# The first loads of a two-layer encoder trunk split over two DMA queues, with matmuls of ones ahead of its first product

## The chip, the core and the metric

The kernel runs on one core of one Trainium2 chip. The metric is the device time of one execution in microseconds (us). Three runs of the kernel before the change took 1084.82, 1081.86 and 1082.02 us, so the median is 1082.02 us. A further execution was recorded by the hardware profiler; it took 1083.18 us, of which 1081.4 us are the span from its first to its last instruction, so that 1.78 us lie around the span.

## What is computed

Two layers of an encoder over 256 tokens with 1024 channels. Each layer applies a gated feed-forward block, a mixer with two groups of heads (neighbourhood attention and a gated long convolution), a second feed-forward block and an input embedding that goes through a gate. The change touches only what happens ahead of, and in, the first feed-forward block of the first layer:

```python
def swiglu(h, w_gate, w_up, w_down):
    return (jax.nn.silu(h @ w_gate) * (h @ w_up)) @ w_down

for i in range(DEPTH):
    x = x + 0.5 * swiglu(rmsnorm(x, g_ffa[i]), w_ffa_gate[i], w_ffa_up[i], w_ffa_down[i])
    u = rmsnorm(x, g_mix[i]) @ w_in[i]
    ...
return rmsnorm(x, g_final)
```

## The kernel before

**Layout.** Channels lie on the 128 partitions and tokens along the free axis. The input x is eight chunks of 128 channels by 256 tokens, 128 KB each, in tiles `x0` to `x7`. Every weight of both layers comes as one long stream of pieces of 1 MB, `w[n]`, each holding 16 tiles of 128x128. A piece is loaded into a `raw` buffer (three of them) by `load()`, and is then cut in two halves of eight tiles by `part()`. The first four pieces are called w0, w1, w2 and so on here.

**Two products for one.** Each weight and each activation is split into a rounded part and a rest. ACT makes the rounded part of a weight half (`wh`, line L281), and DVE subtracts it from the raw weights to get the rest (`wl`, L283). For the input, ACT multiplies chunk c by its gain (`xg`, L1193) and DVE writes the rest behind it (L1196). PE then does one matmul of `wh` with both parts of the activation side by side (512 columns, L188) and, later, one of `wl` with the rounded part alone (256 columns, L197). Six buffers each hold `wh` and `wl`, so ACT and DVE run at most six halves ahead of PE.

**The first block.** The first four halves (w0 and w1) hold the tiles of four output blocks at once, in the order of the chunks: a quarter of a piece is the four tiles that belong to one chunk. PE does eight matmuls of L188 for two chunks, then eight of L197 for the same, four times over. Then come w2, w3, w4 and so on with two output blocks each, 16 matmuls of L188 and 16 of L197 a piece.

**The norm.** The division by the root mean square is applied after the product. ACT squares the eight chunks (L348), POOL adds the squares into `acc` in seven additions, one after the other (L351), and PE sums over the partitions with four small matmuls (L413). DVE takes the sums from there (L421) into a chain of small operations that ends in two scaled identity matrices (L428 feeds ACT's L433), and PE spreads the result over the partitions at L436.

**What sets the order.** PE and ACT run in the order in which the program is written: a fibre per piece of side work is advanced after every few matmuls. The order on DVE, POOL and SP is chosen by a scheduler when the kernel is built. All engines run their own rows strictly in order. All loads are issued from SP's queue. A load takes one of eight completion semaphores in turn, and waits until the load that used it before has landed, so eight loads can be under way.

**The lines to follow.** SP issues the gains and other small columns (`sm`, L251), then w0 in quarters (L253) with `x0` to `x3` between them (L254), then `x4` to `x7` (L257, L259) around two halves of w1 (L258), then whole pieces (L261). ACT's first work is the load of a table for its functions and a dummy activation (L223). The loop at L1188 to L1196 writes the first eight chunks' work in order.

Of the kernel before, what the change touches and what calls it, by code (L numbers as in the profile page):

```python
# [11 lines left out]
F32 = mybir.dt.float32  # L12
# [6 lines left out]
P = 128  # L19
T = 256  # L20
D = 1024
DEPTH = 2
KD = D // P
# [4 lines left out]
EPS = 1e-6  # L28
HALF = 8
GROUP = 24  # L30

E = mybir.EngineType
ORDERED = {E.PE,E.Activation}
# [44 lines left out]
def hybrid_trunk(ctx: ExitStack, tc: tile.TileContext, w, xT, pT, rpb, small, gfin, wf, zT, dft, idft, decay, out):  # L78
    nc = tc.nc
    V, S, G, PE = nc.vector, nc.scalar, nc.gpsimd, nc.tensor  # L80

    cp = ctx.enter_context(tc.tile_pool(name="const", bufs=1))
# [13 lines left out]
    def nm(s):  # L96
        uid[0] += 1
        return f"{s}{uid[0]}"
# [4 lines left out]
    def t2(dt=F32, s="t"):  # L103
        return k2.tile([P, 512], dt, tag="k2", name=nm(s))
# [7 lines left out]
    def f(ap):  # L112
        return ap.bitcast(F32)
# [66 lines left out]
    class Wide:  # L180
# [6 lines left out]
        def mm(cls, b, lh, ll, r, start, stop, last):  # L187
            PE.matmul(b, lh, r, start=start, stop=False)  # L188
            cls.later.append((b[:, T:], ll, r[:, :T], stop))
            if last or len(cls.later) == GROUP:  # L190
                cls.flush()
# [18 lines left out]


    sm = cp.tile([P, DEPTH * NCOL], F32, name="sm")
    x = [cp.tile([P, T], F32, name=f"x{c}") for c in range(KD)]

    def col(i, c):
        return sm[:, i * NCOL + c : i * NCOL + c + 1]
# [2 lines left out]
    V.memset(onesf, 1.0)  # L219
    ones = cp.tile([P, P], F32R, name="ones")  # L220
    V.tensor_copy(ones, onesf)
    warm = sp.tile([P, 2], F32, tag="warm", name="warm")
    S.activation(warm, onesf[:, 0:2], AF.Silu)  # L223
    ident = cp.tile([P, P], F32, name="ident")
# [19 lines left out]
    def load():  # L244
        n = Stream.loaded
        if n >= DEPTH * PIECES:
            return
        raw = rawp.tile([P, 16, P], F32, tag="raw", name=nm("raw"))
        src = w[n].rearrange("p (a b) -> p a b", b=P)
        if n == 0:  # L250
            nc.sync.dma_start(sm, small)  # L251
            for q in range(4):
                nc.sync.dma_start(raw[:, 4 * q : 4 * q + 4], src[:, 4 * q : 4 * q + 4])  # L253
                nc.sync.dma_start(x[q], xT[q])  # L254
        elif n == 1:
            for q in range(2):
                nc.sync.dma_start(x[4 + 2 * q], xT[4 + 2 * q])  # L257
                nc.sync.dma_start(raw[:, q * HALF : (q + 1) * HALF], src[:, q * HALF : (q + 1) * HALF])  # L258
                nc.sync.dma_start(x[5 + 2 * q], xT[5 + 2 * q])  # L259
        else:  # L260
            nc.sync.dma_start(raw, src)  # L261
        Stream.raws[n] = raw
        Stream.loaded += 1

    def part(steps=1):

        n = Stream.parted
        Stream.parted += 1
        while Stream.loaded < min(n // 2 + 2, DEPTH * PIECES):
            load()  # L270
        raw = Stream.raws[n // 2]
        h = whp.tile([P, HALF, P], F32R, tag="wh", name=nm("wh"))
        l = wlp.tile([P, HALF, P], F32R, tag="wl", name=nm("wl"))
        fb = Fiber(None)
        Stream.ready[n] = (h, l, fb)

        def go():
            k = HALF // steps
            for a in range(0, HALF, k):
                src = raw[:, n % 2 * HALF + a : n % 2 * HALF + a + k]  # L280
                S.copy(h[:, a : a + k], src)  # L281
                yield
                V.tensor_sub(l[:, a : a + k], src, f(h[:, a : a + k]))  # L283
            if n % 2:
                Stream.raws.pop(n // 2)
                load()

        fb.gen = go()
        return fb
# [892 lines left out]


    load()
    load()
    first = [part(2), part(2), part(), part()]
    hls = [t2(F32R, "xg") for _ in range(KD)]
    for c in range(KD):  # L1188
        g = col(0, C_FFA + c)
        fb = first[c // 2]  # L1190
        if c % 2 == 0 or c < 4:
            fb.step()
        S.activation(hls[c][:, :T], x[c], AF.Copy, scale=g)  # L1193
        if c % 2:
            fb.finish()
        V.scalar_tensor_tensor(hls[c][:, T:], x[c], g, f(hls[c][:, :T]), op0=ALU.mult, op1=ALU.subtract)  # L1196
# [24 lines left out]
def _constants():  # L1221


    n = 2 * T
    ang = 2.0 * np.pi * (np.outer(np.arange(T), 2 * np.arange(P) + 1) % (2 * n)) / (2 * n)
    re, im = np.cos(ang), -np.sin(ang)
    dft = np.concatenate([re, im], axis=1).reshape(P, 2, T).transpose(1, 0, 2).astype(np.float32)
    sign = 1.0 - 2.0 * (np.arange(T) % 2)
    idft = (np.stack([re.T, re.T * sign, im.T, im.T * sign]) * (2.0 / n)).astype(np.float32)

    tl = np.linspace(0.0, 1.0, T, dtype=np.float32)
    wv = (np.float32(2.0 * math.pi) * np.arange(T, dtype=np.float32) / np.float32(T)).astype(np.float32)
    fb = np.linspace(1e-4, 15.0, 16, dtype=np.float32)
    fw = (fb[None, :] * wv[:, None]).astype(np.float32)
    order = np.arange(T).reshape(P, 2).T.ravel()
    zT = np.zeros((P, T), np.float32)
    zT[:33] = zT[64:97] = np.concatenate([tl[:, None], np.cos(fw), -np.sin(fw)], axis=1)[order].T
    deltas = np.abs(np.linspace(math.log(1e-2) / 1.5, math.log(1e-2) / 0.3, HY, dtype=np.float32))
    decay = np.exp(-tl[:, None] * deltas[None, :]).astype(np.float32)[order].reshape(2, P, HY)
    return dft, idft, zT, decay  # L1240


def _rpb_index():

    r, c = np.arange(T) // 64, np.arange(T) % 64
    lo = np.clip(c - 8, 0, 48)[:, None]
    ok = (c[None] >= lo) & (c[None] < lo + 16)
    at = (r[None] - r[:, None] + 7) * 31 + np.clip(c[None] - c[:, None] + 15, 0, 30)
    return np.where(ok, at, 15 * 31).reshape(2, P, T).transpose(1, 0, 2)
# [49 lines left out]
def _layout(a):  # L1299
    small = np.zeros((P, DEPTH * NCOL), np.float32)  # L1300

    def cols(v):
        return v.reshape(-1, P).T

    for i in range(DEPTH):
        b = i * NCOL
        for c, name in ((C_FFA, "g_ffa"), (C_MIX, "g_mix"), (C_OUT, "g_out"), (C_FFB, "g_ffb"), (C_PLE, "g_ple")):
            small[:, b + c : b + c + 8] = cols(a[name][i])
        for j in range(3):
            small[:, b + C_SC + 12 * j : b + C_SC + 12 * (j + 1)] = cols(a["w_sc"][i, j])  # L1310
        small[:, b + C_BSC : b + C_BSC + 12] = cols(a["b_sc"][i])
        small[:, b + C_HYB : b + C_HYB + 4] = cols(a["hy_bias"][i])
        for j, name in enumerate(("b_f1", "b_f2", "b_f3", "filt_freq")):
            small[:64, b + C_BF + j] = small[64:, b + C_BF + j] = a[name][i]
    wf = np.zeros((DEPTH, P, 3 * P + 2 * HY), np.float32)
    for i in range(DEPTH):
        for j, name in enumerate(("w_f1", "w_f2", "w_f3")):
            v = a[name][i]
            for r in (0, 64):
                for c in (j * P, j * P + 64):  # L1320
                    wf[i, r : r + len(v), c : c + 64] = v
        wf[i, :64, 3 * P :] = wf[i, 64:, 3 * P :] = a["w_f4"][i]
    padded = np.full((DEPTH, NH, 15 * 31 + 1), -1e30, np.float32)
    padded[:, :, :-1] = a["na_rpb"].reshape(DEPTH, NH, 15 * 31)
    rpb = padded[:, :, _rpb_index()]
    dft, idft, zT, decay = _constants()
    return {
        "w": _weights(a),
        "xT": a["x"][0].T.reshape(KD, P, T),
        "pT": a["p"][:, 0].transpose(0, 2, 1),  # L1330
        "rpb": rpb,
        "small": small,
        "gfin": np.broadcast_to(a["g_final"], (P, D)),
        "wf": wf,
        "zT": zT,
        "dft": dft,
        "idft": idft,
        "decay": decay,
    }
# [17 lines left out]
```

## Time and profile before

The profile gives the busy time of each engine in the span, the share of what ended last, and the memory traffic:

| what | value |
|---|---|
| median of three runs | 1082.02 us |
| profiled execution | 1083.18 us |
| its span | 1081.4 us |
| DVE busy | 875.0 us (81%) |
| ACT busy | 659.4 us (61%) |
| POOL busy | 129.9 us (12%) |
| moved from memory | 192.38 MB, 179 GB/s over the span |
| PE's first matmul | 6.77 us after the start of the span |

An engine that is busy all the time is not by that alone the bound, since a matmul counts as busy while it streams at whatever rate the clock allows. So the rows to read beside the busy time are those of waits: which engine stood idle, before which line, and whose end released it. In the timeline, a row is a run of equal instructions: start, busy time, engine, line, what is written and read, and how many.

### The profile page before, as it was taken

The numbers are of one execution on the slowest core, as the hardware profiler recorded it, in microseconds if no ns is written. First come the engines' busy times: TensorE is split into PE (matmuls) and PEld (weight loads), VectorE is DVE, ScalarE is ACT, GpSimd is POOL, SyncE is SP. The second block draws the span as 40 slices with busy tenths as digits, with TensorE's granted clock in tenths as the row PEclk, the third lists the DMA queues.
The fourth block names the chain that finished last, engine by engine and source line by source line (L and its number), as shares of the span: only waits on it lengthen the run. The fifth ranks groups of instructions, "written<-read, shape, count | busy, mean of one in ns | idle before, by whom it ended". The sixth has DMA issues, their size and how long they took to land. (4 is left out here: it accounts for less than half of the span.)

```text
span 1081.4 us, 17162 instructions
## 1 busy us (share of the span) xinstructions
PE 1058.3 (98%) x6442; PEld 948.2 (88%) x6442; DVE 875.0 (81%) x1562; ACT 659.4 (61%) x1198; POOL 129.9 (12%) x138
## 2 busy tenths in 40 slices
PE   7999999999989999999999999999999999999996
PEld 6888888899978888888988888889999788888885
DVE  5999878798987877766789888899989787776765
ACT  7666555476755756555667665655767566564553
POOL 3000111502213000010110001223131200000100
PEclk9999999999999999999999999999999999999998
DMA  8666545464344555555455654545523455555541
GB/s 320 220 225 234 196 156 195 175 213 139 117 166 153 198 195 186 183 177 195 157 208 194 233 188 166 192 156 182 200 88 114 169 181 200 181 184 190 169 163 39
DMA packets 33411, 194.54 MB, mean 180 GB/s; under 512 B 3632, under 2 KB 6832, under 8 KB 11312
## 3 DMA queue, kind: packets, MB, share of 16 engines
q1 hardware_dynamic: 33328, 193.44, 51.8%
q8 instruction: 51, 0.84, 0.3%
q14 instruction: 32, 0.26, 0.1%
HBM read 192.38 MB, written 1.05 MB: 179 GB/s over the span
## 5 line engine op out<-in xcount | busy, mean ns | idle before, releaser
L283 DVE TENSOR_TENSOR wl<-raw,wh 128x1024 fp32r<-128x1024 f32 (+1 forms) x350 | 430.8, 1253 | 109.0 <-ACT wh L281 53.8
L281 ACT CAST wh<-raw 128x1024 fp32r<-128x1024 f32 (+1 forms) x350 | 363.5, 1043 | 186.7 <-PE ps L188 91.6
L188 PE MATMUL ps<-xg,wh 128*128 128x512 f32 x1408 | 345.1, 394 | 13.3 <-DVE xg L1196 6.8
L188 PEld LDWEIGHTS ps<-xg,wh 128*128 128x128 f32 x1408 | 258.7, 189 | 64.3 <-DVE xg L365 8.0
L197 PEld LDWEIGHTS ps<-xg,wl 128*128 128x128 f32 x1408 | 181.5, 191 | 7.6
L197 PE MATMUL ps<-xg,wl 128*128 128x256 f32 x1408 | 183.8, 283 | 0.0
L188 PE MATMUL ps<-act,wh 128*128 128x512 f32 x704 | 173.0, 391 | 0.0
L188 PEld LDWEIGHTS ps<-act,wh 128*128 128x128 f32 x704 | 128.2, 189 | 23.8
L351 POOL TENSOR_TENSOR acc<-acc,q 128x256 f32<-128x256 f32 x56 | 55.7, 994 | 537.2 <-ACT q L348 401.8
L167 PE MATMUL ps<-xg,wh 128*128 128x256 f32 x384 | 109.1, 284 | 0.0
L169 PE MATMUL ps<-xg,wl 128*128 128x256 f32 x384 | 108.7, 283 | 0.0
L168 PE MATMUL ps<-xg,wh 128*128 128x256 f32 x384 | 108.6, 283 | 0.0
L197 PEld LDWEIGHTS ps<-act,wl 128*128 128x128 f32 x704 | 92.9, 191 | 5.1
L197 PE MATMUL ps<-act,wl 128*128 128x256 f32 x704 | 94.4, 282 | 0.0
L202 ACT COPY gu<-ps 128x256 f32<-128x256 f32 x176 | 56.4, 375 | 45.1 <-PE ps L197 45.0
L167 PEld LDWEIGHTS ps<-xg,wh 128*128 128x128 f32 x384 | 73.7, 192 | 0.1
L168 PEld LDWEIGHTS ps<-xg,wh 128*128 128x128 f32 x384 | 73.7, 192 | 0.1
L169 PEld LDWEIGHTS ps<-xg,wl 128*128 128x128 f32 x384 | 73.7, 192 | 0.0
L205 DVE TENSOR_TENSOR gu<-gu,ps 128x256 f32<-128x256 f32 x176 | 66.2, 415 | 0.0
L500 DVE TENSOR_TENSOR act<-s,act 128x256 fp32r<-128x256 f32 x88 | 36.6, 425 | 33.1 <-ACT act L498 32.4
L363 ACT ACTIVATE xg<-x,sm 128x256 fp32r<-128x256 f32 x56 | 27.0, 505 | 38.4 <-DVE x L529 24.3
L365 DVE SCALAR_TENSOR_TENSOR xg<-x,sm,xg 128x256 fp32r<-128x256 f32 x56 | 29.7, 550 | 12.6 <-ACT xg L363 12.4
(209 smaller groups left out, 1236.4 us busy)
## 6 DMA issues: line engine op xcount, KB each, us to landing
raw<-in_w SPq DMA_DIRECT2D x172, 1024.0 KB, 4.9
bias<-in_rpb SPq DMA_DIRECT2D x16, 256.0 KB, 2.7
raw<-in_w SPq DMA_DIRECT2D x4, 256.0 KB, 4.4
x<-in_xT SPq DMA_DIRECT2D x8, 128.0 KB, 4.6
raw<-in_w SPq DMA_DIRECT2D x2, 512.0 KB, 5.7
t<-in_wf SPq DMA_DIRECT2D x4, 256.0 KB, 5.3
dec<-in_decay SPq DMA_DIRECT2D x4, 256.0 KB, 5.4
out<-yo SPq DMA_DIRECT2D x3, 256.0 KB, 2.1
```

Of the source, the lines that this page charges most:

```text
L167: PE.matmul(o, lh, rh, start=start, stop=False)
L168: PE.matmul(o, lh, rl, start=False, stop=False)
L169: PE.matmul(o, ll, rh, start=False, stop=stop)
L188: PE.matmul(b, lh, r, start=start, stop=False)
L197: PE.matmul(o, ll, rh, start=False, stop=stop)
L202: S.copy(dst, b[:, T:])
L205: V.tensor_add(dst, dst, b[:, :T])
L281: S.copy(h[:, a : a + k], src)
L283: V.tensor_sub(l[:, a : a + k], src, f(h[:, a : a + k]))
L351: G.tensor_add(self.ac, self.ac, q)
L365: V.scalar_tensor_tensor(hl[:, T:], x[c], g, f(hl[:, :T]), op0=ALU.mult, op1=ALU.subtract)
L500: V.tensor_sub(hl[:, T:], s, f(hl[:, :T]))
```

## The change

Three things are changed. The small columns and x are loaded from ACT's queue, x in four pieces of two chunks (256 KB) into one tile, ahead of ACT's table load. SP's queue carries weights alone, with w0 and w1 both in quarters. PE gets eleven matmuls of a constant matrix of ones, 512 columns wide, into a bank that nothing reads; they wait only for the ones. As a consequence of the quarters of w1, ACT and DVE split its two halves in steps of a quarter as they do for w0.

```diff
+WARM = 11
...
-    x = [cp.tile([P, T], F32, name=f"x{c}") for c in range(KD)]
+    xs_all = cp.tile([P, KD * T], F32, name="x")
+    x = [xs_all[:, c * T : (c + 1) * T] for c in range(KD)]
...
     V.tensor_copy(ones, onesf)
+
+    idle = bank()
+    for _ in range(WARM):
+        PE.matmul(idle, ones, ones.unsqueeze(1).to_broadcast([P, 4, P]), start=True, stop=True)
+    nc.scalar.dma_start(sm, small)
+    for q in range(4):
+        cs = slice(2 * q * T, 2 * (q + 1) * T)
+        nc.scalar.dma_start(xs_all[:, cs], xT[:, cs])
     warm = sp.tile([P, 2], F32, tag="warm", name="warm")
     S.activation(warm, onesf[:, 0:2], AF.Silu)
...
-        if n == 0:
-            nc.sync.dma_start(sm, small)
+        if n < 2:
             for q in range(4):
                 nc.sync.dma_start(raw[:, 4 * q : 4 * q + 4], src[:, 4 * q : 4 * q + 4])
-                nc.sync.dma_start(x[q], xT[q])
-        elif n == 1:
-            for q in range(2):
-                nc.sync.dma_start(x[4 + 2 * q], xT[4 + 2 * q])
-                nc.sync.dma_start(raw[:, q * HALF : (q + 1) * HALF], src[:, q * HALF : (q + 1) * HALF])
-                nc.sync.dma_start(x[5 + 2 * q], xT[5 + 2 * q])
         else:
             nc.sync.dma_start(raw, src)
...
-    first = [part(2), part(2), part(), part()]
+    first = [part(2) for _ in range(4)]
...
-        if c % 2 == 0 or c < 4:
-            fb.step()
+        fb.step()
...
-        "xT": a["x"][0].T.reshape(KD, P, T),
+        "xT": a["x"][0].T.reshape(KD, P, T).transpose(1, 0, 2).reshape(P, KD * T),
```

On PE and on ACT nothing else moves: behind these rows the order is that of before. The lines of the changed kernel are numbered two or three higher (L281 becomes L284, L283 becomes L286, L421 becomes L424).

ACT's first rows before the change, from the start of the program; `wh3` is the first half of w0 and `xg12`, `xg13` are the scaled chunks 0 and 1:

```order
L223 ACT_TABLE_LOAD
L223 ACTIVATE warm_97<-onesf_93 128x2
L281 CAST wh3_131<-raw1_114 128x512
L1193 ACTIVATE xg12_141<-x0_85,sm_84 128x256
L281 CAST wh3_131<-raw1_114 128x512
L1193 ACTIVATE xg13_142<-x1_86,sm_84 128x256
```

And ACT's first rows in the changed kernel:

```order
L228 DMA sm_84<-in_small 128x192
L231 DMA x_85<-in_xT 128x512 x4
L233 ACT_TABLE_LOAD
L233 ACTIVATE warm_107<-onesf_86 128x2
L284 CAST wh4_134<-raw2_124 128x512
L1195 ACTIVATE xg13_144<-x_85,sm_84 128x256
```

Five loads now stand ahead of the table load; the fourth load of x takes the semaphore of `sm` and so waits for `sm` to have landed.

DVE's rows before the change from the first half of w2 on; `wl25` and `wl23` are the halves of w2, `wl35` and `wl40` those of w3, `wl46` and `wl56` those of w4, and `v68` is what L421 takes from the norm's sums:

```order
L283 TENSOR_TENSOR wl25_184<-raw7_135,wh24_183 128x1024
L283 TENSOR_TENSOR wl23_182<-raw7_135,wh22_181 128x1024
L283 TENSOR_TENSOR wl35_220<-raw20_164,wh34_219 128x1024
L283 TENSOR_TENSOR wl40_249<-raw20_164,wh39_248 128x1024
L421 TENSOR_SCALAR v68_376<-ps67_373 128x2
L386 TENSOR_SCALAR rt69_378<-v68_376 128x2
L387 TENSOR_SCALAR rt71_380<-v68_376 128x2
L388 TENSOR_SCALAR rt70_379<-rt69_378 128x2
L283 TENSOR_TENSOR wl46_280<-raw21_178,wh45_279 128x1024
L283 TENSOR_TENSOR wl56_308<-raw21_178,wh55_307 128x1024
```

And the same place in the changed kernel, where `wl47` and `wl57` are the halves of w4, `wl60` and `wl67` those of w5:

```order
L286 TENSOR_TENSOR wl36_227<-raw21_167,wh35_226 128x1024
L286 TENSOR_TENSOR wl41_256<-raw21_167,wh40_255 128x1024
L286 TENSOR_TENSOR wl47_287<-raw22_185,wh46_286 128x1024
L286 TENSOR_TENSOR wl57_315<-raw22_185,wh56_314 128x1024
L206 TENSOR_TENSOR gu51_309<-gu51_309,ps30_195 128x256
L206 TENSOR_TENSOR gu50_308<-gu50_308,ps29_194 128x256
L206 TENSOR_TENSOR gu49_307<-gu49_307,ps28_193 128x256
L206 TENSOR_TENSOR gu48_306<-gu48_306,ps27_192 128x256
L286 TENSOR_TENSOR wl60_333<-raw33_210,wh59_332 128x1024
L286 TENSOR_TENSOR wl67_370<-raw33_210,wh66_369 128x1024
L424 TENSOR_SCALAR v69_383<-ps68_380 128x2
```

The scheduler has moved the norm's row (L421, now L424) behind the halves of w4 and w5 and four additions of results; before, these stood behind it. Later on DVE some 20 rows of the filter's small operations change places with rows beside them, and on SP two loads of biases go behind two pieces of weights.

## The prediction

> **What bounds the kernel now.** I read the page's busy times and its chain first, then PE's waits, then the timeline of the first 40 us.
>
> ```profile
> PE 1058.3 (98%) x6442; PEld 948.2 (88%) x6442; DVE 875.0 (81%) x1562; ACT 659.4 (61%) x1198; POOL 129.9 (12%) x138
> PE 19%; DVE 1%; ACT 0%; issue 0%; DVEq 0%; ACTq 0%
> PE ps L188 <- DVE xg L1196: 6.8, 1, 6.8
> PE ps L188 <- DVE xg L365: 6.5, 4, 3.0
> PE ps L413 <- POOL acc L351: 0.2, 1, 0.2
> ```
>
> PE is busy for 98% of the span, and the chain that ended last is nearly all PE as far as it is followed. The last three rows (total, times, longest) hold all PE waits that matter: 6.8 us before the first matmul, four waits of 6.5 us in all at later seams, and 0.2 us at L413, where PE wants the sums of squares that POOL adds. So a microsecond won at the start arrives at the end if PE keeps it past L413. The later seams hang on PE's own results and move along with it.
>
> ```profile
> 6.77 3.52 PE L188 MATMUL ps<-xg,wh 128*128 128x512 f32 x8 [6.77 <-DVE xg L1196]
> 11.08 2.00 PE L188 MATMUL ps<-xg,wh 128*128 128x512 f32 x8
> 14.08 2.12 PE L188 MATMUL ps<-xg,wh 128*128 128x512 f32 x8
> 19.78 3.82 PE L188 MATMUL ps<-xg,wh 128*128 128x512 f32 x16
> 25.34 1.55 PE L188 MATMUL ps<-xg,wh 128*128 128x512 f32 x6
> 27.14 0.61 PE L413 MATMUL ps<-onesf,acc 128*128 128x1 f32 x4 [0.25 <-POOL acc L351]
> 38.42 0.28 PE L436 MATMUL ps<-s,ones 128*128 128x256 f32 x1
> ```
>
> The first eight matmuls take 3.52 us, the next eight of the same shape 2.00 us: PE begins at about half its rate. The half rate has a row of its own elsewhere, behind a long idle stretch (columns: stretch and length, PE, PEld, DVE, ACT, POOL, granted clock, DMA share, GB/s):
>
> ```profile
> 320.80:323.87 3.07, 0.05 (x2) 0.02 (x1) 3.07 (x8) 3.07 (x8) 0.26 (x1) 1.00 0.05 19
> 323.87:327.28 3.41, 3.41 (x12) 2.92 (x13) 1.52 (x3) 0.27 (x1) 3.10 (x3) 0.50 0.32 89
> 852.94:856.35 3.41, 1.67 (x8) 1.09 (x7) 3.41 (x10) 3.29 (x9) 0.82 (x2) 1.00 0.58 228
> ```
>
> After 3.0 us without a matmul the clock was 0.50 for 3.41 us, which costs half of that, 1.71 us. A stretch of 3.41 us with PE busy for 1.67 us left it at 1.00. The clock column is not to be trusted at the very start, where the durations say half and it says 1.00.
>
> **Part 1: the ones.** They replace idle time.
>
> ```profile
> 1.03 0.35 DVE L221 CAST ones<-onesf 128x128 fp32r<-128x128 f32 x1
> 4.98 0.62 ACT L281 CAST wh<-raw 128x512 fp32r<-128x512 f32 x1 [2.75 <-DMA raw<-in_w]
> 5.50 0.50 ACT L1193 ACTIVATE xg<-x,sm 128x256 fp32r<-128x256 f32 x1
> 6.24 0.48 DVE L1196 SCALAR_TENSOR_TENSOR xg<-x,sm,xg 128x256 fp32r<-128x256 f32 x1
> ```
>
> The ones are ready at 1.38 us. Eleven matmuls at 3.52/8 = 0.44 us end at 6.2 us, ahead of the first scaled chunk (6.24 + 0.48 = 6.72), so they delay nothing; if that chunk came at 5.7 they would cost 0.5 us. The half rate lasted some 3 to 3.5 us at either place, so 4.8 us of ones should end it. The gain on PE is 3.52 - 2.00 = **1.5 us**, less 0.25 us because chunk 1 is not ready earlier. The Trainium skill (TensorE: Matmul & The Clock Gate, Part 1) says that the gate looks at free-running windows of about 3.4 us, so the cold time varies from run to run; by it this term would be anything from the 1.5 us of this profile to half of two windows, an estimate of 3.4 us. The 3.41 us row agrees with the window's length.
>
> **Part 2: the loads.** SP issued one load each 0.47 us, and w0's first quarter second (the row of `sm` ends with its KB and the us from issue to landing):
>
> ```profile
> 0.74 0.39 SPq L251 DMA_DIRECT2D sm<-in_small  x1
> 1.18 0.42 SPq L253 DMA_DIRECT2D raw<-in_w  x1
> 1.65 0.42 SPq L254 DMA_DIRECT2D x<-in_xT  x1
> sm<-in_small SPq DMA_DIRECT2D x1, 96.0 KB, 2.0
> 0.73 1.28 ACT L223 ACT_TABLE_LOAD   x1 [0.73 <-PEq L1347]
> 1.50:6.77 5.27, 0.00 (x0) 0.00 (x0) 1.09 (x2) 2.29 (x6) 0.00 (x0) 1.00 0.75 228
> 6.77:9.85 3.08, 3.08 (x7) 2.48 (x8) 2.53 (x5) 2.53 (x6) 0.00 (x0) 1.00 0.98 341
> 16.23 2.00 ACT L281 CAST wh<-raw 128x1024 fp32r<-128x1024 f32 x2 [0.98 <-DMA raw<-in_w]
> ```
>
> That quarter is now issued 0.44 us earlier, but the first chunk of x now comes with the second, 128 KB more; at 228 GB/s that is 0.57 us. I put the first scaled chunk at no change, within 0.4 us either way. No row shows an issue on ACT; the nearest is SP's 0.42 us. Four of these end at 2.4, the fifth waits for `sm` (0.74 + 2.0 us to landing = 2.74), then table load 1.28 and dummy 0.2 end at 4.7, under the cast at 4.98: hidden, with 0.3 us to spare. If an issue took double, all of the first chunks would be late by 1.5 us; if it took nothing, nothing is won.
>
> Up to w2, 4.29 MB have to come (x, w0, w1 and w2 with 1.05 MB each, and `sm`), and ACT waited for w2 until 16.23. Early the engines moved 228 GB/s at a share of 0.75, later 341 at 0.98. Two queues can fill that early gap: 5.27 us at 341 instead of 228 would move 0.6 MB more, or 1.7 us. No row shows two queues; between nothing and 1.7 us I take **1.2 us**, so w2 at 15.0. The Trainium skill (DMA: Bandwidth & Descriptors, Issuing engines are not separate DMA queues) speaks against this part: queues share the same engines and a second one saves only issue time. By it w2 would land only some 0.4 us earlier; no row here can decide.
>
> With data no longer late at 14.08, PE needs for each pair of chunks what it needed from 11.08 to 14.08 less the wait there, 2.8 us. From 6.77 four pairs and the 0.25 us for chunk 1 end at 18.2; from w2's start to the end of the six matmuls ahead of L413 it took 25.34 + 1.55 - 19.78 = 7.1 us. PE would so be at L413 at about **25.4** instead of 26.9.
>
> **Part 3: what is late next.** L413 waits for POOL, and POOL for ACT's squares, which stand on ACT behind the two casts of w2.
>
> ```profile
> 18.45 0.71 ACT L348 ACTIVATE q<-x 128x256 f32<-128x256 f32 x2
> 18.93 8.15 POOL L351 TENSOR_TENSOR acc<-acc,q 128x256 f32<-128x256 f32 x7 [17.63 <-ACT q L348]
> 18.93:23.85 4.92, 4.92 (x29) 4.27 (x28) 3.20 (x3) 4.83 (x10) 4.74 (x3) 1.00 0.95 356
> 23.85:27.10 3.25, 3.04 (x20) 2.44 (x19) 0.00 (x0) 2.71 (x6) 2.94 (x4) 1.00 0.98 345
> 22.68 2.00 ACT L281 CAST wh<-raw 128x1024 fp32r<-128x1024 f32 x2
> 27.79 0.16 DVE L421 TENSOR_SCALAR v<-ps 128x2 f32<-128x2 f32 x1 [4.55 <-PE ps L413]
> 36.93 0.70 ACT L433 ACTIVATE s<-ident,rl 128x128 fp32r<-128x128 f32 x2 [8.08 <-DVE rl L428]
> ```
>
> The seven additions fall in two stretches. While DVE subtracts weights (three times), an addition takes 4.92/3 = 1.64 us; while DVE stands still, 3.25/4 = 0.81 us. DVE stands still there because L421 waits 4.55 us for L413 with w4's halves queued behind it. The change turns these around: w4's two subtractions no longer wait, and come as soon as ACT has cast w4 (22.68 to 24.68 before). POOL is then still adding. Starting 1.2 us earlier, at 17.7, with five held-up additions and two free ones, it ends at 17.7 + 5 x 1.64 + 2 x 0.81 = **27.5** (27.1 before). With three held up it would be 25.9, with six 28.4. I take five, since w4's two halves are two more than the three of before. So PE, ready at 25.4, stands for 2.1 us and does L413 at 27.55 instead of 27.14. The Trainium skill (SBUF — State Buffer, Who interferes with whom) states the rule behind it: a DVE instruction with two SBUF inputs and a GpSimd one that reads SBUF lock each other out of a shared port. The two rates above agree.
>
> Behind L413 nothing is won back: PE streams without a wait to 320 us. DVE's chain from L413 to L436 is relieved rather than pressed: in the old order it ended in ACT's L433 at 37.6, 0.8 us ahead of PE's L436 at 38.42, after an 8.08 us wait; with w4's and w5's halves done beforehand it has only its small operations left. Eleven rows more on PE, four more half-size subtractions and the moved bias loads lie beside PE's work.
>
> **Sum.** Against the profiled execution: -1.5 (rate) +0.25 (chunk 1) -0.25 (data at 14.08), all taken back at L413, which ends at +0.4 us: 1083.18 + 0.4 = 1083.6. That execution holds a stretch at half clock (1.71 us), without which it is 1081.5; two of the three runs, at 1081.86 and 1082.02, can only have been without it. So I predict 1081.5 + 0.4 = **1081.9 us**, practically the median of before.
>
> **The rivals.** (a) POOL is not slowed: w4's halves come later than its last additions, or the additions slip between them. It ends at 25.9, L413 comes 1.2 us earlier than before, and the time is 1080.3. For it: the additions alone take 7 x 0.81 = 5.7 us. Against: even with three held up POOL is at it until 25.9, and ACT's first cast of w4 ends at 22.68 + 1.05 = 23.7 if it does not move at all. (b) Slower: the new idle stretch before L413, 2.1 us, brings the half clock back, as 3.0 us did at 320; 1.67 us busy of 3.41 did not. It decides between 1.74 and 3.0 us of idleness, and costs 1.71 us: 1083.6. (c) Two queues bring nothing and w2 stays at 16.2: POOL starts at 18.9 and ends at 28.7, +1.6: 1083.1. ACT late by its issues has the same end. (d) The ones do not raise the clock: PE is at L413 at 26.9 instead of 25.4, still ahead of POOL, and the time is again 1081.9. The time alone would not show it.
>
> **How the numbers follow.** My forecast with (d) gets 0.47, (a) 0.27, (b) 0.15, (c) 0.11. The range runs from (a) less 0.3 us for the first chunk, 1080.0, to (b) with a late chunk, 1084.2; outside lies a run with two half-clock stretches. A measurement here can tell 0.3% (3.2 us) from no change. No case reaches 1078.8; I leave 0.06 for a longer half rate at the start of the runs of before than I think, 0.04 for a second stretch at half clock, and 0.90 for no difference.
>
> **What would show it.** The first real group of eight matmuls should take 2.0 to 2.3 us, from 6.4 to 7.1 on; ACT's first cast of w2 near 15.0; POOL's first addition near 17.7 and its last ending near 27.5, with five of them over 1.2 us; PE idle some 2 us before L413 (now L416), released by POOL. If L413 comes by 26, (a) holds; if a clock of 0.50 follows it, (b). I am wrong if another wait of PE before 40 us exceeds 0.5 us, or if PE's seams after 300 us change by more than that.

## The result and the profile after

The change makes the kernel about 2 us slower. That is less than 0.3%, but the time lies above the prediction's range.

| | before | after |
|---|---|---|
| median of 22 runs each | 1083.47 us | 1085.86 us |
| lowest to highest | 1081.32 to 1085.14 | 1082.31 to 1087.37 |
| after / before | | 1.0019 [1.0013, 1.0026] |
| profiled execution | 1083.18 us | 1086.25 us |
| first matmul of L188 (L189 after) | 6.77 us | 8.33 us |
| POOL's seven additions end | 27.09 us | 29.06 us |
| norm's sums on PE, L413 (L416 after) | 27.14 us | 29.33 us |
| PE stops for 3.0 us, first seam | 320.83 us | 322.91 us |

The last row is used as **the mark** from here on: from L416 to it PE streams without a wait, so it shows what the head of the program costs, without the clock's accidents further on. It moved by 2.1 us, about as much as L416 did (2.2 us), so in these two executions nothing is lost between L416 and the mark. Behind the mark they differ by another 1.0 us; that is time at half clock, as the windows below show.

PE's timeline of the changed kernel (start, length, engine, line and operation, what is written and read, and how many; in brackets the idle time before it and what ended that):

```profile
1.44 5.06 PE L227 MATMUL ps<-ones 128*128 128x512 f32 x11 [1.44 <-DVE ones L223]
8.33 3.78 PE L189 MATMUL ps<-xg,wh 128*128 128x512 f32 x8 [1.83 <-DVE xg L1198]
13.62 2.39 PE L189 MATMUL ps<-xg,wh 128*128 128x512 f32 x8
27.94 1.56 PE L189 MATMUL ps<-xg,wh 128*128 128x512 f32 x6
29.33 0.50 PE L416 MATMUL ps<-onesf,acc 128*128 128x1 f32 x4
```

The ones run to 6.50 us, where 6.2 was forecast. Then PE waits 1.83 us more for the first scaled chunk, and its first eight matmuls still take 3.78 us, the half rate. It reaches L416 at 29.3 us without a further wait. Why the chunk is late stands in ACT's timeline, and in the row of DMA issues for `sm` (which ends with KB and us to landing):

```profile
0.73 0.40 ACTq L228 DMA_DIRECT2D sm<-in_small  x1
1.16 3.95 ACTq L231 DMA_DIRECT2D x<-in_xT  x4
5.15 1.28 ACT L233 ACT_TABLE_LOAD   x1 [5.15 <-DMA sm<-in_small]
6.55 0.60 ACT L284 CAST wh<-raw 128x512 fp32r<-128x512 f32 x1
15.40 2.00 ACT L284 CAST wh<-raw 128x1024 fp32r<-128x1024 f32 x2 [1.31 <-DMA raw<-in_w]
sm<-in_small ACTq DMA_DIRECT2D x1, 96.0 KB, 4.0
```

The load of `sm` landed 4.0 us after its issue, twice the 2.0 us it took at the head of SP's queue, when that was the only one. The fourth load of x stands on ACT until then, and the table load behind it begins at 5.15 us, so ACT's first cast is at 6.55 instead of 4.98. From there 8.33 is as far as 6.77 was from 4.98. The row at 15.40 is the cast of w2, which has come earlier than before.

Why the rate did not rise stands in windows of 3.41 us, counted back from the moment at which the clock's record begins to say 1.00 in this execution, 14.43 us (length, busy time of PE, PEld, DVE, ACT and POOL with the number of instructions, granted clock, DMA share, GB/s):

```profile
0.78:4.19 3.41, 2.75 (x7) 2.17 (x8) 0.52 (x2) 0.00 (x0) 0.45 (x2) 1.00 0.62 145
4.19:7.60 3.41, 2.31 (x6) 1.29 (x4) 0.41 (x1) 2.44 (x5) 0.00 (x0) 1.00 0.97 351
7.60:11.02 3.42, 2.69 (x6) 2.15 (x7) 3.42 (x8) 3.42 (x8) 0.00 (x0) 1.00 1.04 394
11.02:14.43 3.41, 3.41 (x13) 3.03 (x12) 3.41 (x8) 3.06 (x7) 0.00 (x0) 1.00 1.04 404
325.04:328.45 3.41, 2.52 (x8) 2.03 (x9) 1.97 (x4) 1.18 (x4) 2.63 (x2) 0.50 0.25 34
328.45:331.87 3.42, 3.42 (x14) 3.03 (x14) 2.63 (x7) 1.67 (x5) 0.73 (x1) 0.50 0.69 278
```

The stretch of half clock at 325.04 begins 310.61 us after 14.43, which is 91 times 3.413 us: the windows run through from the start. In none before 11.02 was PE busy throughout (81%, 68% and 79%); the first that it fills is followed by the full rate. At the seam the same happens again: a window with 74% leaves the clock at half, so two windows are lost instead of one. The trace has no record of the clock ahead of 14.43, and the column prints 1.00 there, where the durations say half.

POOL's additions, and three windows across them:

```profile
18.10 10.96 POOL L354 TENSOR_TENSOR acc<-acc,q 128x256 f32<-128x256 f32 x7 [16.80 <-ACT q L351]
18.10:26.40 8.30, 8.30 (x48) 7.20 (x47) 6.86 (x8) 7.74 (x16) 7.95 (x5) 1.00 0.95 347
26.40:27.20 0.80, 0.80 (x9) 0.80 (x8) 0.68 (x3) 0.80 (x1) 0.73 (x1) 1.00 1.12 205
27.20:29.10 1.90, 1.90 (x14) 1.68 (x12) 1.87 (x2) 0.73 (x3) 1.80 (x1) 1.00 0.84 336
```

POOL starts 0.83 us earlier than before and ends 1.97 us later, at 29.06. Five additions take 7.95 us while DVE subtracts weights, the sixth takes 0.73 while DVE adds results out of PE's banks (L206), the seventh 1.80 beside the next subtraction. So at L416 two delays of the same size meet: PE's own (29.33) and POOL's (29.06). Which of them costs the time, this one profile can't say.

### The profile page after: what moved, and what is told of

Its sections match the earlier page's. It is cut to its first block, busy times and chain, and to the rows that moved or that the text cites. A ratio compares the mean times of both kernels' runs of the same rounds, so it can differ in the third digit from the quotient of the medians.

```text
span 1084.5 us, 17192 instructions
## 1 busy us (share of the span) xinstructions
PE 1065.3 (98%) x6453; PEld 953.9 (88%) x6453; DVE 878.8 (81%) x1564; ACT 661.0 (61%) x1200; POOL 132.9 (12%) x138
## 5 line engine op out<-in xcount | busy, mean ns | idle before, releaser
L286 DVE TENSOR_TENSOR wl<-raw,wh 128x1024 fp32r<-128x1024 f32 (+1 forms) x352 | 431.2, 1249 | 112.0 <-PE ps L198 53.8
L284 ACT CAST wh<-raw 128x1024 fp32r<-128x1024 f32 (+1 forms) x352 | 364.0, 1038 | 188.7 <-PE ps L189 94.7
L189 PE MATMUL ps<-xg,wh 128*128 128x512 f32 x1408 | 346.6, 395 | 8.4 <-DVE xg L368 6.5
L189 PEld LDWEIGHTS ps<-xg,wh 128*128 128x128 f32 x1408 | 259.6, 190 | 60.0 <-DVE xg L368 8.0
L189 PE MATMUL ps<-act,wh 128*128 128x512 f32 x704 | 173.0, 391 | 0.0
L189 PEld LDWEIGHTS ps<-act,wh 128*128 128x128 f32 x704 | 128.2, 189 | 23.8
L206 DVE TENSOR_TENSOR gu<-gu,ps 128x256 f32<-128x256 f32 x176 | 65.9, 414 | 0.0
```

Source lines behind the costliest of these rows:

```text
L206: V.tensor_add(dst, dst, b[:, :T])
```

## The experiments

Each kernel ran some eleven times (e1 seven) beside runs of the kernel before; the ratios have 95% intervals. Lines are those of the changed kernel, and a few numbers off where an edit shifts them. The expectations speak of two theories. By **A** the loss comes from ACT's stop on its own loads, which makes the first matmul late. By **P** POOL's longer chain holds L416 as well, so that relieving one side leaves the other. All compute the whole reference; the ones go into a bank that nothing reads.

| kernel | first L189 | POOL ends | L416 (wait) | mark | median us | ratio to before |
|---|---|---|---|---|---|---|
| after | 8.33 | 29.06 | 29.33 (0) | 322.91 | 1085.86 | 1.0019 [1.0013, 1.0026] |
| e1: three loads on ACT | 7.11 | 29.01 | 29.06 (2.76) | 324.27 | 1086.31 | 1.0029 [1.0019, 1.0040] |
| e2: L416 later | 8.43 | 28.70 | 34.22 (0) | 321.77 | 1082.28 | 0.9999 [0.9988, 1.0009] |
| e3: e1 and e2 | 6.95 | 28.95 | 32.20 (0) | 319.75 | 1081.66 | 0.9984 [0.9975, 0.9992] |
| e4: no ones | 8.15 | 29.93 | 29.99 (1.28) | 323.64 | 1085.61 | 1.0021 [1.0009, 1.0033] |
| e5: old loads, ones, L416 later | 6.66 | 29.92 | 33.03 (0) | 320.57 | 1082.50 | 0.9991 [0.9982, 1.0000] |
| e6: old loads, ones | 6.30 | 27.39 | 27.44 (0.61) | 321.13 | 1083.41 | 1.0004 [0.9995, 1.0013] |
| e7: old loads, L416 later | 6.58 | 28.94 | 32.90 (0) | 320.45 | 1082.77 | 0.9998 [0.9989, 1.0007] |
| e8: e1, squares early | 6.87 | 17.20 | 27.13 (0) | 320.72 | 1082.72 | 0.9996 [0.9987, 1.0005] |
| e9: two x loads on each queue, L416 later | 7.01 | 28.62 | 31.45 (0) | 319.01 | 1081.19 | 0.9985 [0.9977, 0.9994] |
| e10: e9 without ones | 7.07 | 28.82 | 32.94 (0) | 320.48 | 1082.76 | 0.9999 [0.9990, 1.0008] |
| e11: e2 with 16 ones | 8.29 | 28.50 | 32.61 (0) | 320.15 | 1082.33 | 0.9994 [0.9986, 1.0003] |

Mark, waits and starts are of one profiled execution each, with its own position of the clock's windows; the median and ratio are of many.

**e1: ACT's stop taken away.** x comes in three loads instead of four, so that none waits for a semaphore in use.

```diff
-    for q in range(4):
-        cs = slice(2 * q * T, 2 * (q + 1) * T)
+    for lo, hi in ((0, 2), (2, 4), (4, 8)):
+        cs = slice(lo * T, hi * T)
```

> x comes in three loads on ACT instead of four, so that no load on ACT reuses the semaphore of sm and ACT does not stop ahead of its table load. Mark: the start of PE's 3 us idle stretch near 320 us (320.83 before, 322.91 after the change), which holds all that the head gained or lost. Theory P (two causes, each alone enough: PE starts late, and POOL's seven additions end near 29 us because DVE's w4 rows lock them out): first real matmul near 7.0 instead of 8.33, yet POOL still ends at 28.5 to 29.3 and PE now idles 1.5 to 3 us before L416; mark at 322.3 to 323.0, no gain against the changed kernel. Theory A (the stop of ACT is the whole loss): L416 at 27.6 to 28.0 and the mark near 321.3.

ACT's stop is gone, and the first matmul is at 7.11. But the time is not better. ACT's and PE's timelines and two windows of this kernel:

```profile
2.61 1.28 ACT L233 ACT_TABLE_LOAD   x1 [2.61 <-issue]
4.64 0.62 ACT L284 CAST wh<-raw 128x512 fp32r<-128x512 f32 x1 [0.53 <-DMA raw<-in_w]
24.75 1.55 PE L189 MATMUL ps<-xg,wh 128*128 128x512 f32 x6
29.06 0.61 PE L416 MATMUL ps<-onesf,acc 128*128 128x1 f32 x4 [2.76 <-POOL acc L354]
27.21:30.63 3.42, 1.57 (x9) 1.40 (x10) 3.42 (x8) 0.12 (x1) 1.72 (x2) 1.00 0.71 285
30.63:34.04 3.41, 3.41 (x12) 2.83 (x11) 2.98 (x16) 0.45 (x2) 0.00 (x0) 0.50 0.85 281
```

PE is ready for L416 at 26.30, 3.0 us earlier than in the changed kernel, and stands for 2.76 us until POOL's last addition at 29.01. The stop leaves it busy for 1.57 us of a window of 3.42, and the next window is granted half the clock. So the mark is even later, 324.27; no expectation for this kernel had the half clock in it. A alone falls: with ACT's stop gone, POOL takes its place and costs more.

**e2: L416 later.** The constant says how many of PE's steps pass before the norm's sums are taken; their place in PE's order moves behind the next matmuls, some 5 us later.

```diff
-STAT_F = 8
+STAT_F = 14
```

> The changed kernel with the norm's matmuls (L416) 34 rows later on PE (STAT_F 14 instead of 8), so that PE is some 6 us later there and POOL's end near 29 us can hold nothing. Theory P: PE is late by itself (first real matmul 8.33, half rate until 14.4 in the changed kernel), so the mark near 320 stays at 322.3 to 323.0. Rival (POOL's additions are the whole loss): the mark comes back to 320.8 to 321.4.

The first matmul is as late as in the changed kernel, yet the whole loss is gone from the time: 0.9999 instead of 1.0019. The mark, 321.77, lies between the two ranges of the expectation, 0.5 us under that of theory P and 0.4 us above the rival's. The two windows that decide the head in this execution:

```profile
5.85:9.27 3.42, 1.26 (x6) 0.67 (x4) 1.98 (x4) 3.41 (x8) 0.00 (x0) 1.00 1.00 356
9.27:12.68 3.41, 3.41 (x13) 2.86 (x12) 3.41 (x8) 3.25 (x8) 0.00 (x0) 0.50 1.08 422
```

Here the ones had raised the clock by 5.85, and the wait of 2.16 us behind them lowered it again (PE busy 1.26 of 3.42 us), until 12.68 instead of 14.43. So PE is earlier than in the profiled execution of the changed kernel by the position of the windows alone, and with L416 at its old place, behind the six matmuls that end at about 28.2, it would have waited for POOL (28.70). How long the head runs at half rate thus differs from execution to execution. POOL's end differs less: in the four profiled kernels with these loads it lies at 28.50 (e11), 28.70 (e2), 29.06 (after) and 29.93 (e4). In the changed kernel it holds L416 in every execution whose PE would be earlier, and a long stop can bring the half clock with it, as in e1.

How often that happens can be read, in part, from the mean granted clock of every run. In the 93 runs of before that were measured beside the experiments, a lower clock goes with a longer time: 27 runs have 0.997 and took 1081.5 to 1082.4 us, 14 have 0.994 and took 1084.4 to 1085.3. In the changed kernel 13 of 22 runs have 0.994 or less, in e1 6 of 7, in e2 only 2 of 12. The changed kernel's mean is 0.9943 and that of before 0.9957, a difference worth some 1.5 us; e2's is 0.9952. So more than half of the loss is time at half clock behind the clock's first rise, and moving L416, which leaves the loads, the ones and POOL's additions as they were, takes away most of the runs of that kind. That this half clock stands right behind L416 in the runs without a profile is inferred from that, not seen.

**e3: both.**

> Both edits together: three loads of x on ACT and L416 34 rows later. Theory P: neither hold-up is left; first real matmul near 7.0, full rate by 8, PE without a wait to the mark, which lies at 319.0 to 320.0, that is 3 to 4 us earlier than in the changed kernel and 1 to 1.8 earlier than before the change. Theory A or POOL alone: no better than the better one of the two single edits, 320.8 or later.

The mark is 319.75, 3.2 us under the changed kernel's and 1.1 us under that of before, and the ratio, 0.9984 [0.9975, 0.9992], is under 1. PE's timeline:

```profile
6.95 2.30 PE L189 MATMUL ps<-xg,wh 128*128 128x512 f32 x8 [0.45 <-DVE xg L1198]
32.20 0.50 PE L416 MATMUL ps<-onesf,acc 128*128 128x1 f32 x4
```

Now the ones do what they can: they run to within 0.45 us of the first real matmul, and the first eight take 2.30 us. Both delays are real. ACT's stop shows in the time only when POOL no longer holds L416: alone its removal gains nothing (e1), behind e2 it gains another 0.0015, though the intervals of e2 and e3 overlap a little.

**e4: no ones.** `WARM = 0`, all else as changed.

> The changed kernel without the eleven matmuls of ones, loads as changed. Theory P with the clock's free-running windows: the ones ended 1.83 us ahead of the first real matmul and no window before 11.0 was busy enough, so they bought nothing in the profiled run; without them first real matmul at 8.3, full rate between 11.5 and 15, mark at 322.3 to 323.5, no difference to the changed kernel over 0.1%. Rival (the ones do raise the clock in most runs and the loss comes from elsewhere): slower than the changed kernel by 1 us or more.

The first eight take 3.78 us as with the ones, the mark is 0.1 us above the range, and at L416 PE waits 1.28 us for POOL, which ends later here (29.93). The time, 1.0021, is that of the changed kernel: in it the ones buy nothing. The loss is put together differently, though: e4's mean granted clock, 0.9956, is nearly that of before (0.9957), so little of its loss is half clock behind the first rise.

**e6 and e7: what lengthens POOL's chain.** Both have the loads of before. e6 adds the ones to the kernel before, and the scheduler leaves DVE's order alone; e7 is the kernel before with STAT_F 14 only, and the scheduler moves w4's subtractions ahead of L421, as in the change.

```diff
 e6
+WARM = 11
...
+    idle = bank()
+    for _ in range(WARM):
+        PE.matmul(idle, ones, ones.unsqueeze(1).to_broadcast([P, 4, P]), start=True, stop=True)
 e7
-STAT_F = 8
+STAT_F = 14
```

> The kernel before plus the ones alone; DVE's order stays that of before, with L421 ahead of w4's halves. If POOL's end is the floor, POOL's last addition ends at 27.0 to 27.2 as before, PE idles 1.2 to 1.7 us ahead of L413, which starts at 27.1 to 27.2, and the mark stays at 320.7 to 320.9; no half clock behind so short a stop; time 0 to 0.1% under before. Rival (POOL is no floor): L413 near 25.7 and the mark near 319.4. Against the changed kernel it tells what DVE's order is worth: POOL's end 2 us earlier here.

> The kernel before with L413 34 rows later alone. Only the 0.25 us wait for POOL and the small-matmul rows go: mark 320.4 to 320.7, time 0 to 0.05% under before. If instead the later place is worth a microsecond by itself (by the DVE's order or the chain behind it), the mark is at 319.8 or earlier and the reading of the two-by-two runs falls.

The chain's second part in e6 and then in e7, as windows:

```profile
24.20:27.40 3.20, 2.63 (x17) 2.03 (x15) 0.00 (x0) 2.28 (x7) 2.94 (x4) 1.00 0.99 376
```

```profile
23.95:28.95 5.00, 5.00 (x31) 4.39 (x30) 4.74 (x7) 4.00 (x8) 4.70 (x4) 1.00 0.94 319
```

The last four additions take 2.94 us with DVE at rest and 4.70 with DVE busy; the chain is 8.14 us long in e6 and 9.91 in e7. Neither new loads nor ones are needed for that; DVE's order is. (The kernel before has 8.15.) e6 also shows that the ones alone gain nothing with L416 where it was: PE stands 0.61 us for POOL, L413 is 0.3 us later than before, and the ratio is 1.0004. Three of its forecasts were missed by a little: POOL's end (27.39) and the mark (321.13) came 0.2 us late, and PE stood less than the 1.2 to 1.7 us expected, since it had lost 1.4 us before to waits for chunks 1 and 4. e7's was as expected, and moves the time by nothing.

**e5: ones on the old loads, with L416 out of the way.** This is e6 with STAT_F 14.

> The kernel before with its loads untouched, plus the eleven matmuls of ones and L413 34 rows later on PE. If what the ones bring is 1.2 to 1.5 us of PE's rate, and it is lost only where PE then has to wait for POOL, the first real matmul stays at 6.8, its group of eight takes 2.0 to 2.4 us instead of 3.5, PE does not wait before 320 us, and the mark (start of the idle stretch near 320) is at 319.0 to 319.6 instead of 320.83; time 0.1 to 0.25% under before. Rival (the loads on two queues are what made the best kernel so far faster, not the ones): mark at 320.4 or later, time within 0.05% of before.

The mark falls short of the expectation by a microsecond (320.57) and is where the rival put it; the time, 0.09% under before, lies between the two. PE's timeline:

```profile
8.37 1.20 PE L189 MATMUL ps<-xg,wh 128*128 128x512 f32 x4 [0.52 <-DVE xg L1201]
14.36 2.11 PE L189 MATMUL ps<-xg,wh 128*128 128x512 f32 x8 [1.06 <-DVE xg L1201]
```

At the full rate PE runs into the data of the old loads, at chunk 1 and at chunk 4. Against e7, the same without ones, the mark is no better: what the ones gain is given back to the loads.

**e8: the squares taken early.** e1, with each chunk's square on ACT right behind its scaling, so that POOL is done long before L416.

```diff
+    new_norm()
     for c in range(KD):
...
+        Norm.sq.add(x[c])
...
...
-    new_norm()
-    early.append(spawn(squares()))
```

> The changed kernel with three loads of x on ACT and the eight squares taken inside the first loop, one behind each scaled chunk, so that POOL's additions start near 8 us instead of 18 and are done long before L416 (at its old place). If POOL's lateness is what holds PE, L416 starts without a wait at 25.8 to 26.6, and the mark is at 319.3 to 320.2, as with L416 moved; time 0.1 to 0.2% under before. Rival (L416's place itself, or the idle clock, is the cost): a wait of over 1 us ahead of L416 stays, or the mark stays at 321.5 or later.

POOL ends at 17.20 and L416 doesn't wait. But it is at 27.13 and the mark at 320.72, both 0.5 us later than expected, as PE waits more often for the chunks, between which ACT's squares now stand. The row of PE's waits (total, times, longest):

```profile
PE ps L189 <- DVE xg L1199: 1.9, 4, 1.1
```

The 2.76 us of e1 are gone, the waits in the head are 1.9 us instead of e1's 0.9, and the ratio is 0.9996 [0.9987, 1.0005].

**e9 and e10: the version with the best mark, and the ones' worth in it.** ACT loads only the first two pieces of x; SP loads the others ahead of the quarters of w1 that need them.

```diff
-    for q in range(4):
+    def load_x(queue, q):
         cs = slice(2 * q * T, 2 * (q + 1) * T)
-        nc.scalar.dma_start(xs_all[:, cs], xT[:, cs])
+        queue.dma_start(xs_all[:, cs], xT[:, cs])
+
+    load_x(nc.scalar, 0)
+    load_x(nc.scalar, 1)
...
+                if n == 1 and q % 2 == 0:
+                    load_x(nc.sync, 2 + q // 2)
...
-STAT_F = 8
+STAT_F = 14
```

> A version meant to beat both: of x only the first two pieces go by ACT's queue, the other two stand on SP's queue between the weights' quarters (x4 and x5 ahead of w1's first quarter, x6 and x7 ahead of its third), L416 34 rows later. Nothing on ACT waits for a semaphore; the later chunks of x no longer take room from w0's third and fourth quarters, whose lateness cost the version with three loads 0.52 us at chunk 3. Theory P: first real matmul 6.7 to 7.0, no wait over 0.3 us before 320, mark at 319.0 to 319.6; time 0.15 to 0.3% under before. Rival (the order of the loads is worth nothing more): mark at 319.7 to 320.2 as with three loads on ACT.

> The same without the ones: what the ones are worth where neither POOL nor ACT's stop holds PE. First real matmul at 6.7 to 7.0, its group of eight 3.3 to 3.8 us, the mark 1.2 to 3 us later than with the ones (320.2 to 322), as the clock rises 3.1 to 6.5 us after the first matmul. Rival (the data's arrival hides the half rate): mark within 0.4 us of that with the ones.

The first eight matmuls, in e9 and then in e10 (e9 with `WARM = 0`):

```profile
7.01 2.30 PE L189 MATMUL ps<-xg,wh 128*128 128x512 f32 x8 [0.51 <-DVE xg L1203]
```

```profile
7.07 3.73 PE L189 MATMUL ps<-xg,wh 128*128 128x512 f32 x8 [7.07 <-DVE xg L1203]
```

With data in time and L416 out of the way the ones are worth 3.73 - 2.30 = 1.43 us at once, 1.47 us at the mark and 1.6 us in the medians (1082.76 to 1081.19); eight of e9's eleven runs are faster than e10's fastest, 1081.25. e9 is, with e3, the fastest here and beats both kernels: 0.9985 [0.9977, 0.9994] against before.

**e11: more ones.** e2 with `WARM = 16`, which closes the wait behind the ones from the other side.

> The changed kernel with L416 34 rows later and sixteen ones instead of eleven, so that they reach the first real matmul at 8.4. If the 1.8 to 2.2 us between the ones and the first real matmul is what lets the clock stay or fall back to half rate, then the eight first matmuls take 2.0 to 2.4 us and the clock does not fall before 320; mark at 320.2 to 321.0, against 321.77 with eleven. Rival (the gap is harmless): mark within 0.3 us of 321.8 and time as with eleven.

```profile
1.44 6.38 PE L227 MATMUL ps<-ones 128*128 128x512 f32 x16 [1.44 <-DVE ones L223]
8.29 2.18 PE L189 MATMUL ps<-xg,wh 128*128 128x512 f32 x8 [0.46 <-DVE xg L1198]
```

The first matmul is as late as in e2, but at full rate: 2.18 us, where e2's profiled execution has 3.09 and the changed kernel's 3.78. The mark is 1.6 us under e2's. In the medians nothing is to be seen of it (1082.28 and 1082.33, overlapping intervals): the profile has the expected mechanism, the time is the rival's.

## Why the prediction was wrong

The forecast was 1081.9 us, and no difference beyond 0.3%. The difference, +0.19%, is within that bound. The time, 1085.86, lies 4.0 us above the forecast and 1.7 above the range. Of the 4.0 us, 2.0 were in the starting point. The prediction took 1081.5, an execution free of half clock, since two of its three runs were; 22 runs have a median of 1083.47, and only 27 of the 93 mentioned under e2 have the clock of 0.997 that goes with such times. The other 2.0 us are the change, forecast at +0.4 and measured at 2.4. The term that failed most there is POOL's end (Part 3): with L416 moved out of its way (e2) the time is that of before, though Parts 1 and 2 failed as well and stay so in e2.

**Part 2 failed at "hidden, with 0.3 us to spare".** The step took the landing of `sm`, 2.0 us, over from the old loads, where it was first on the only queue. On ACT's queue, with w0's quarters coming on SP's, it took 4.0 (3.8 to 4.1 in all nine traces with it there), and the 2 us more made ACT's first cast 1.57 us late. So "no change, within 0.4 us" for the first scaled chunk became +1.56. That a fifth issue waits for `sm` had been seen; its price was taken from a row with other traffic. e1 shows the step by itself: with three loads the table load starts at 2.61 and the first matmul at 7.11, which is within the 0.4 us forecast. That the other queue's traffic slowed `sm` is argued, not shown: no run had `sm` on ACT's queue with SP's idle. Fewer loads of x behind it do not help, as it took 3.9 and 4.0 us with two (e9, e10). w2 was forecast for 15.0. ACT's first cast of it came at 15.40, but in three more profiles with the same loads at 15.22 (e2), 15.90 (e11) and 16.49 (e4); with the old loads four profiles have 16.23 to 16.54. The means are 15.75 and 16.39, so some 0.6 us were gained, half of the 1.2 forecast. The Trainium skill (DMA: Bandwidth & Descriptors, Issuing engines are not separate DMA queues) has a second queue save issue time only, put at 0.4 us in the prediction; with profiles that differ by more than a microsecond, these runs can't tell the two apart.

**Part 1 failed at "4.8 us of ones should end it".** There were 5.06 us of ones, but the sum of their lengths does not matter: PE must be busy for most of a window, whose start can lie anywhere, and the gap behind the ones counts against it. In the profiled execution windows of 81%, 68% and 79% before 11.02 left the rate at half; in e2's the rate rose at 5.85 and fell again at 9.27; 85% (e9) raised it. The Trainium skill (TensorE: Matmul & The Clock Gate, Part 1) calls these windows free-running, and the 91 whole windows between two of the clock's changes agree. So in the profiled execution rival (d) held, but because of the gap, and not at its price: it had PE at L413 at 26.9, and PE came at 29.33, as the late chunk came on top. With the gap at 0.5 us (e3, e9, e11) the first eight take 2.18 to 2.30 us; in the time this gain is shown by e9 against e10 alone.

**Part 3 had the right mechanism and too small a size.** POOL was held up as described, by subtractions that the moved order brings forward (e6 against e7). The term "five held-up and two free" measured six and one, and the six together 9.75 us, 1.63 each, as forecast, with one of 0.73 (adding from the windows: 7.95 + 1.80 and 0.73); with the gaps between them the chain is 10.96 long. It started at 18.10, not 17.7, and ended at 29.06, where 27.5 was forecast: 0.4 us by the start, 0.8 by the sixth held-up addition, 0.3 by the gaps. "With six 28.4" stood there as a case; I chose five because w4's two halves are two more, and left out that additions slowed this much reach into w5's halves as well. Five does occur: the profiles of e7, e10 and e11 have five, with chains of 9.89 to 9.91 us, and those of the changed kernel and of e1 to e5 and e9 have six.

**Rival (b) is real, but not in the profiled execution of the changed kernel.** It was priced at a stop of 2.1 us. That execution has no stop at L416, as PE is late itself. With that removed (e1) the stop is 2.76 us and the half clock comes as rival (b) says, at 46% busy, and the granted clocks listed under e2 say that runs of the changed kernel that were not profiled lose time at half clock too. Rival (a) did not happen, as POOL was slowed. Of (c), w2 came earlier in the profiled execution; ACT late by its issues did happen, but not with the end given there: it held PE's first matmul and not POOL's start.

**The sum failed by its form.** It added up a PE that was early and then stopped by POOL. In the profile PE was late by 1.56 us at the first matmul and by 1.0 more through the half rate (8 + 8 matmuls from 8.33 to 13.62, 5.29 us, where before 4.31 sufficed), and so came to L416 with POOL. The loss at the mark, 2.1 us, has two causes side by side, of which e2 and e3 together take away the one and then the other.

What stays open: where the half clock lies in the runs without a profile. The changed kernel with DVE's old order was not tried, since the order comes from the scheduler; e6 and e7 show the order's effect with the old loads only. And e3 and e9 can't be told apart in time.

## What to carry to other kernels

A load's landing time belongs to the queue and the traffic it was measured with: take it over to another queue only with a margin, and count loads that an engine issues itself against the semaphores they reuse, for an engine that waits to issue does nothing else. Warming matmuls paid here only where they ran to within 0.5 us of the first real one and nothing held PE behind it (e9 against e10). Before a start is made earlier, look at what the next common point waits for on all its sides, and move that point first (e2 costs one constant); where two delays of the same size meet there, undoing one alone can bring nothing or a loss (e1), and undoing the other can hide that the first is still there (e2). And take a starting time from many runs, as three were off by 1.45 us here.

## What the hardware showed unexpectedly

- The clock is judged in windows of 3.413 us that run through the execution: in all thirteen traces, every stretch at the full rate between two changes of the clock is a whole number of them (91 after the change, 92 before, 7 and 86 in e1). Busy shares from 68 to 81% left the clock at half; 85% (e9, 3.78 to 7.19 us: 2.90 us busy) and 90% raised it (before, 6.43 to 9.85 us: 3.08 us busy), as did full ones. 46% (e1) and 37% (e2) lowered it, 49% (before, at 852.94) did not.
- Each window at half clock that PE fills costs 1.71 us, and a 3.0 us stop meets one such window, or two, or none (the profiles of before, after and e3 at the first seam). The times of one kernel step accordingly: the 22 runs of before lie at 1081.3 to 1082.3 (6), 1083.0 to 1083.9 (10) and 1084.6 to 1085.1 (6). That the steps are these windows fits the granted clocks listed under e2, which fall from 0.997 to 0.994 over the same times; one window more is 0.0016.
- An addition of 128x256 on POOL took 0.73 us free and 1.6 to 1.8 us beside DVE's subtraction of two operands of 128x1024; beside DVE's additions that take one operand from PE's banks it took 0.73 us as well. The Trainium skill (SBUF — State Buffer, Who interferes with whom) says that a DVE instruction with at most one SBUF input, outside the modes that use both ports, does not contend with GpSimd, and this agrees.
